# Gathering 64 more columns of v, splitting the weights of two blocks at once, and own homes for the first raw tile and the row of norms, in a streaming-encoder trunk

## The chip, the cores and the metric

The kernel runs as one program on one core of a Trainium2 chip. The metric is device microseconds of one execution. TensorE (PE) does the matmuls and transposes, VectorE (DVE), ScalarE (ACT) and GpSimd (POOL) the rest; SyncE (SP) issues most of the DMAs, POOL issues the gathers that take their row numbers from memory.

## The reference

256 tokens of width 2048 pass one layer: a convolution and an S5 state space side by side, a cross attention to 256 memory tokens, then a PEER layer and a last RMSNorm. The change lies in PEER and what follows it:

```python
def peer(h, w_q, sub_keys, u_tab, v_tab):
    q = (h @ w_q)...                               # 8 heads, two halves each
    ...                                            # two top-16 per head, top-16 of their 256 sums
    idx = ...                                      # 8 heads x 16 experts of 16384 per token
    g = jax.nn.softmax(top_s, axis=-1)
    u = jnp.take(u_tab, it, axis=0)
    act = jax.nn.gelu(jnp.einsum("td,tkd->tk", xt, u))
    v = jnp.take(v_tab, it, axis=0)
    return jnp.einsum("tk,tkd->td", gt * act, v)

out = rms_norm(h + peer(...), final_norm_g)
```

Each token picks 128 of 16384 experts, and an expert is a row of `peer_u` and a row of `peer_v`, both 2048 wide.

## The kernel before

The program is built with a Tile framework whose scheduler sets the order of instructions on each engine by a timeline of its own; pools with a fixed number of buffers and semaphores do the rest. The 256 tokens are two halves of 128 (`tt` = 0, 1). By the trace, mixing and attention run from 0 to about 777 us, the query projection `peer_w_q` to 842, the dot products with u and the routing to about 1533, the stage on v to 2047, and the last norm from there to the end at 2063.

**Dot products with u.** The first 768 columns of all 16384 rows of `peer_u` are read as 128 blocks of 128 rows (`dense()`): SP loads `raw`, PE transposes it (L969), ACT copies it to `ut` (L971), PE multiplies it with `hnT`, the transposed tokens (L975). The other 1280 columns are gathered for the picked rows only (`dot()`): POOL issues 256 gathers (L928), DVE multiplies and sums each (L930). `hnT` is made on POOL by an addition (L798) and a multiplication with `rbf`, the row of norms (L799).

**The stage on v.** The first DC = 1472 columns go through PE: the sparse gate-times-activation weights stand as a dense matrix `W`, two tiles WA and WB (one for each token half) of 128 blocks of 128 x 128. For each block SP loads 128 rows of `peer_v` (`vr`); ACT casts it to fp32r (`vh`, L103) and DVE takes the remainder (`vl`, L104); the block's weights are split in the same way (`wh` on ACT, L1205, `wl` on DVE, L1206, once for WA and once for WB); and PE sums three products (wh·vh L1215, wl·vh L1216, wh·vl L1217) for two halves and three column chunks (512, 512, 448) in PSUM: 18 matmuls a block. The other GC = 576 columns are gathered for the picked rows: 256 gathers on POOL (L1180) into 6 buffers `v`, and for each an accumulation on DVE, `accg = v * coef + accg` (L1182), 128 for the first token half and then 128 for the second. In the text of the program about two gathers stand behind each block:

```python
        while done * NB < (b + 1) * (NTT * NSLOT + 8) and done < NTT * NSLOT:
            next(gathering)
            done += 1
```

**The end.** For each half the matmul sums are added to the residual (L1225, DVE), squared and summed on ACT (L1226, and L1227 for `accg`), reduced (L1228), turned into a reciprocal root (L110, L111), and the four column pieces are scaled (L1234 to L1237) and stored. `accg` of the second half is complete only when its last gathered row is in.

The tile WB is not filled until `dense()`; until then the top of it serves as space for routing tiles, cut off by `host(n)`.

Of the kernel before, what the change touches and what calls it, by code (L numbers as in the profile page):

```python
# [9 lines left out]
F32 = mybir.dt.float32  # L10
F32R = mybir.dt.float32r
# [3 lines left out]
AF = mybir.ActivationFunctionType  # L15
# [5 lines left out]
P = 128  # L21
T = 256
NTT = T // P
# [15 lines left out]
NSLOT = PH * TOPK  # L39
NB = 128  # L40
# [7 lines left out]
DU = KD * P  # L48
DG = D - DU
GROUPS = ((1, 1, 2, 2, 2), (2, 2, 2, 2))  # L50
GC = 576
GU = 64
DC = D - GC
COLS = [slice(c, min(c + 512, DC)) for c in range(0, DC, 512)]
NCH = len(COLS)
VG_BUFS = 6
VR_BUFS = 4
WL_POOL = 0
PQ_COLS = (128, 384, 512)
NWHOLE = 1  # L60
W_IN, W_K, W_V = True, True, True
# [17 lines left out]
def trunk(ctx, tc, a, out, dbg=None):  # L79
    nc = tc.nc  # L80
    V, S, G, PE, SY = nc.vector, nc.scalar, nc.gpsimd, nc.tensor, nc.sync
# [4 lines left out]
    consts = ctx.enter_context(tc.tile_pool(name="consts", bufs=1))  # L86
# [7 lines left out]
    eps_t = consts.tile([P, 1], F32, name="eps_t")  # L94
# [10 lines left out]

    def row_bcast(vec):
        return bass.AP(tensor=vec.tensor, offset=vec.offset, ap=[[0, P], [1, D]])

    def rstd_of(dst, ssq, n):
        S.activation(dst, ssq, AF.Sqrt, bias=eps_t[: dst.shape[0]], scale=1.0 / n)  # L110
# [38 lines left out]
    with ExitStack() as wctx:  # L149
# [71 lines left out]
        def run(g):  # L221
            for _ in g:
                pass
# [5 lines left out]
        with ExitStack() as mctx:  # L229
# [382 lines left out]
            for k in range(CW):  # L612
                for q in range(CQ):
                    src, o = cpad[:, q, k:k + T], accs[q // 4][:, q % 4, :]
# [131 lines left out]
        ffn = wctx.enter_context(tc.tile_pool(name="ffn", bufs=1, side="right"))  # L746
        wb_p = wbx.enter_context(tc.tile_pool(name="wb_p", bufs=1))
        WB = wb_p.tile([P, NB, P], F32, name="WB")
        spare = [NB * P]

        def host(n):
            spare[0] -= n
            return WB.rearrange("p b t -> p (b t)")[:, spare[0]:spare[0] + n]
# [7 lines left out]
        cands = host(2 * TOPK * TOPK)  # L761
        top_r = [host(n * PH * TOPK) for n in (2, 2, 2, 1, 2, 2)]
        sco = [host(PH * 2 * P).rearrange("p (h s n) -> p h s n", h=PH, s=2) for _ in range(NTT)][::-1]
        free_blocks = spare[0] // P

        pq_cols = [(sum(PQ_COLS[:i]), w) for i, w in enumerate(PQ_COLS)]

        def ev_pq(n, half, ps):
# [5 lines left out]
            for sd in range(2):  # L774
# [6 lines left out]
                for tt in range(NTT):  # L781
                    S.activation(sco[tt][:, hh:hh + nh, sd, :], ss[:, tt, :nh], AF.Copy, scale=rstd_f[:, tt:tt + 1])

        run(linear(fT, a["peer_w_q"], 0, PH * P, ev_pq, False, cols=pq_cols))
        r8 = small.tile([P, NTT], F32, name="r8")
        V.tensor_scalar(r8, rstd_f, float(CH), None, op0=ALU.mult)
# [2 lines left out]
        for tt in range(NTT):  # L789
            V.tensor_scalar(dg[:, tt, :], ident, r8[:, tt:tt + 1], None, op0=ALU.mult)  # L790
            PE.matmul(pr[:, tt * P:(tt + 1) * P], ones, dg[:, tt, :], start=tt == 0, stop=tt == 1,
                      skip_group_check=True)
        rbf = ffn.tile([P, T], F32, name="rbf", tag="qp", bufs=2)
        S.copy(rbf, pr)
        for n in range((KD + 3) // 4):
            w = min(KD - 4 * n, 4)
            o = hnT[:, 4 * n:4 * n + w, :]
# [162 lines left out]
    def dense():  # L960
        for b in range(NB):
            if b == NB // 2:
                while (1, len(GROUPS[1]) - 1) not in ready:
                    yield
            raw = lr_d.tile([P, DU], F32, name="raw", bufs=4)
            SY.dma_start(raw, a["peer_u"][b * P:(b + 1) * P, :DU])
            pt = psd.tile([P, KD, P], F32, name="ut")
            for k in range(KD):
                PE.transpose(pt[:, k, :], raw[:, k * P:(k + 1) * P], ident)  # L969
            ut = lr_d.tile([P, KD, P], F32, name="ut", bufs=2)  # L970
            S.copy(ut, pt)  # L971
            if b % 2 == 0:
                ps = psd.tile([P, 2, T], F32, name="sy")
            for k in range(KD):
                PE.matmul(ps[:, b % 2, :], ut[:, k, :], hnT[:, k, :], start=k == 0 and b % 2 == 0,  # L975
                          stop=k == KD - 1 and b % 2 == 1, skip_group_check=True)
            if b % 2:
                S.copy(W[0][:, :, b - 1:b + 1], ps[:, :, :P].rearrange("p b t -> p t b"))
                S.copy(by_token[:, b // (NB // 2), :, (b - 1) % (NB // 2):(b - 1) % (NB // 2) + 2],
                       ps[:, :, P:].rearrange("p b t -> p t b"))  # L980
            yield
# [214 lines left out]

    gathering = gathered()
    done = 0
    for b in range(NB):
        if b == TAIL_AT:  # L1200
            load_tail()
        wh = vs.tile([P, NTT, P], F32R, name="wh")
        wl = vs.tile([P, NTT, P], F32R, name="wl")
        for tt in range(NTT):
            S.copy(wh[:, tt, :], W[tt][:, b, :])  # L1205
            (G if tt < WL_POOL else V).tensor_sub(wl[:, tt, :], W[tt][:, b, :], wh[:, tt, :].bitcast(F32))  # L1206
        vr = vraw_p.tile([P, DC], F32, name="vr")
        SY.dma_start(vr, a["peer_v"][b * P:(b + 1) * P, :DC])
        vh = vs.tile([P, DC], F32R, name="vh")
        vl = vs.tile([P, DC], F32R, name="vl")  # L1210
        split(vh, vl, vr)
        for tt in range(NTT):
            for c, cs_ in enumerate(COLS):
                o = acc[tt][:, c, :cs_.stop - cs_.start]
                PE.matmul(o, wh[:, tt, :], vh[:, cs_], start=b == 0, stop=False)  # L1215
                PE.matmul(o, wl[:, tt, :], vh[:, cs_], start=False, stop=False)  # L1216
                PE.matmul(o, wh[:, tt, :], vl[:, cs_], start=False, stop=b == NB - 1)  # L1217
        while done * NB < (b + 1) * (NTT * NSLOT + 8) and done < NTT * NSLOT:
            next(gathering)
            done += 1  # L1220

    sts = [small.tile([P, NCH + 3], F32, name="rms_st") for _ in range(NTT)]
    for tt, st in enumerate(sts):
# [45 lines left out]
```

## Time and profile before

| | |
|---|---|
| time, three runs | 2063.14, 2064.15, 2064.17 us (median 2064.15) |
| the profiled execution | 2064.74 us, of which the span from first to last instruction is 2063.0 us |
| busy share of the span | PE 95%, PE's weight loads 82%, DVE 82%, ACT 48%, POOL 38% |
| DMA | 571.78 MB, mean 277 GB/s; about 338 GB/s in the v stage |
| last matmul ends, end of span | 2046.95 us, 2063.0 us |

All other times below are in us from the start of the span of that profiled execution. Busy shares are means over very different stages: the v stage alone (1533 to 2047 us) is a quarter of the span, and in its last 16 us PE is idle.

### The profile page before, as it was taken

The page shows a single profiled execution, that of the slowest core. Times are in us where ns is not written, and L with a number is a line of the kernel's source. Part 1 is how long each engine was busy: PE and PEld are TensorE (multiplying, and loading weights), DVE is VectorE, ACT ScalarE, POOL GpSimd, SP SyncE. Part 2 cuts the span into 40 slices and gives each one's busy share as a digit, 9 for nine tenths or more (in the row PEclk, how much of TensorE's full clock was granted, in tenths as well). Part 3 has the DMA queues.
Part 4 walks back from the last instruction along what each step waited for, and adds up shares of the span by engine and source line. Part 5 has one row for each costly group of instructions (what it writes and reads, how often), then busy time and mean ns, then how long its engine had stood idle before and what let it go on. Part 6 is the DMA issues. An engine that isn't in the chain of part 4 may idle for free.

```text
span 2063.0 us, 33320 instructions
## 1 busy us (share of the span) xinstructions
PE 1961.4 (95%) x12361; PEld 1684.1 (82%) x12379; DVE 1683.5 (82%) x2757; ACT 998.2 (48%) x1586; POOL 777.7 (38%) x589
## 2 busy tenths in 40 slices
PE   8899999999999998899999989989999999999996
PEld 7888886786899888788888878867678888888885
DVE  6699999895655557999976666889869899899998
ACT  5775665455544445333333323556564444444444
POOL 1011111000000003444445656453128677677775
PEclk9999999999999999999999999999999999999998
DMA  7888788757855568899999999888539999999996
GB/s 238 204 227 221 202 224 223 226 183 230 276 180 173 168 196 280 273 310 327 318 354 398 406 384 407 282 294 280 172 128 338 364 336 340 343 341 338 337 339 228
DMA packets 203108, 571.78 MB, mean 277 GB/s; under 512 B 31410, under 2 KB 39459, under 8 KB 202818
## 3 DMA queue, kind: packets, MB, share of 16 engines
q1 hardware_dynamic: 135810, 307.48, 44.1%
q0 software_dynamic: 67136, 262.18, 37.8%
q8 instruction: 97, 1.59, 0.3%
q14 instruction: 65, 0.53, 0.1%
HBM read 556.74 MB, written 12.85 MB: 276 GB/s over the span
## 4 chain that ended last, share of the span: by engine, by line
PE 55%; DVE 15%; issue 11%; DMA 9%; POOL 7%; ACT 2%; SPq 0%; POOLq 0%; DVEq 0%; ACTq 0%
PE acc L1216 8%; PE acc L1217 8%; PE acc L1215 8%; POOL u L928 6%; DVE u L930 5%; PE mm L206 4%; PE mm L205 4%; PE mm L207 3%; PE mm L216 3%; PE mm L214 3%; PE mm L215 3%; PE pw L1051 3%; DMA w_lo<-in_w_kv_mem 2%; PE y L1016 1%; DMA xc<-in_mem 1%
## 5 line engine op out<-in xcount | busy, mean ns | idle before, releaser
L1180 POOL DMA_INDIRECT v<-in_peer_v,vidx x256 | 391.2, 1528 | 182.8 <-DVE accg L1182 72.5
L930 DVE SCALAR_TENSOR_TENSOR u<-u,hnF 128x1280 f32<-128x1280 f32 x256 | 387.9, 1518 | 86.2 <-DMA u<-in_peer_u,uidx 85.5
L928 POOL DMA_INDIRECT u<-in_peer_u,uidx x256 | 295.8, 1156 | 330.2 <-DVE u L930 243.3
L975 PE MATMUL sy<-hnT,ut 128*128 128x256 f32 x1536 | 357.6, 385 | 15.4 <-ACT ut L971 15.4
L191 ACT CAST w_hi<-w_raw 128x1024 fp32r<-128x1024 f32 (+2 forms) x228 | 231.3, 1017 | 242.8 <-PE mm L207 118.2
L975 PEld LDWEIGHTS sy<-hnT,ut 128*128 128x128 f32 x1536 | 287.6, 193 | 56.5 <-ACT ut L971 20.7
L196 DVE TENSOR_TENSOR w_lo<-w_raw,w_hi 128x1024 fp32r<-128x1024 f32 (+2 forms) x192 | 226.7, 1183 | 111.4 <-ACT w_hi L191 111.2
L103 ACT CAST vh<-vr 128x1472 fp32r<-128x1472 f32 x128 | 183.3, 1432 | 251.7 <-PE acc L1216 250.2
L1216 PE MATMUL acc<-vh,wl 128*128 128x512 f32 (+1 forms) x768 | 295.4, 385 | 0.3 <-DVE wl L1206 0.3
L1217 PE MATMUL acc<-vl,wh 128*128 128x512 f32 (+1 forms) x768 | 293.7, 385 | 0.1
L216 PE MATMUL mm<-aT_hi,w_lo 128*128 128x256 f32 x960 | 271.9, 290 | 18.8 <-DVE w_lo L196 7.5
L1215 PE MATMUL acc<-vh,wh 128*128 128x512 f32 (+1 forms) x768 | 276.0, 384 | 2.4 <-ACT vh L103 2.4
L214 PE MATMUL mm<-aT_hi,w_hi 128*128 128x256 f32 x960 | 277.1, 291 | 0.8 <-ACT w_hi L191 0.8
L215 PE MATMUL mm<-aT_lo,w_hi 128*128 128x256 f32 x960 | 274.4, 288 | 0.0
L104 DVE TENSOR_TENSOR vl<-vr,vh 128x1472 fp32r<-128x1472 f32 x128 | 216.8, 1694 | 41.9 <-ACT vh L103 41.4
L1182 DVE SCALAR_TENSOR_TENSOR accg<-v,coef,accg 128x576 f32<-128x576 f32 x256 | 208.7, 815 | 6.5 <-DMA v<-in_peer_v,vidx 2.5
L216 PEld LDWEIGHTS mm<-aT_hi,w_lo 128*128 128x128 f32 x960 | 182.8, 193 | 25.2 <-DVE w_lo L196 9.0
L214 PEld LDWEIGHTS mm<-aT_hi,w_hi 128*128 128x128 f32 x960 | 185.7, 194 | 6.6 <-issue 3.7
L215 PEld LDWEIGHTS mm<-aT_lo,w_hi 128*128 128x128 f32 x960 | 186.1, 194 | 3.4 <-issue 2.0
L1216 PEld LDWEIGHTS acc<-vh,wl 128*128 128x128 f32 x768 | 144.6, 188 | 30.9 <-DVE wl L1206 0.7
L1215 PEld LDWEIGHTS acc<-vh,wh 128*128 128x128 f32 x768 | 144.8, 188 | 28.3 <-ACT vh L103 2.6
L1217 PEld LDWEIGHTS acc<-vl,wh 128*128 128x128 f32 x768 | 144.5, 188 | 22.5 <-DVE vl L104 0.9
(383 smaller groups left out, 3187.8 us busy)
## 6 DMA issues: line engine op xcount, KB each, us to landing
vr<-in_peer_v SPq DMA_DIRECT2D x128, 736.0 KB
raw<-in_peer_u SPq DMA_DIRECT2D x128, 384.0 KB
w_raw<-in_w_kv_mem SPq DMA_DIRECT2D x64, 512.0 KB
w_raw<-in_w_in SPq DMA_DIRECT2D x48, 512.0 KB
w_raw<-in_w_out SPq DMA_DIRECT2D x32, 512.0 KB
w_raw<-in_w_q_mem SPq DMA_DIRECT2D x32, 512.0 KB
w_raw<-in_w_o_mem SPq DMA_DIRECT2D x32, 512.0 KB
w_lo<-in_w_kv_mem POOLq DMA_DIRECT2D x24, 512.0 KB, 7.9
```

The source lines that it names most:

```text
L191: S.copy(hi, raw)
L196: V.tensor_sub(lo, raw, hi.bitcast(F32))
L214: PE.matmul(o, wh, ah, start=first and cb % 2 == 0, stop=False, skip_group_check=True)
L215: PE.matmul(o, wh, al, start=False, stop=False, skip_group_check=True)
L216: PE.matmul(o, wl, ah, start=False, stop=last and end, skip_group_check=True)
L928: G.indirect_dma_start(out=u, out_offset=None, in_=a["peer_u"].rearrange("e (q c) -> (e q) c", c=GU), in_offset=bass.IndirectOffsetOnAxis( ...
L930: V.scalar_tensor_tensor(u, u, 1.0, hnF[:, self.tt, :], op0=ALU.mult, op1=ALU.mult, accum_out=self.act[:, j:j + 1])
L975: PE.matmul(ps[:, b % 2, :], ut[:, k, :], hnT[:, k, :], start=k == 0 and b % 2 == 0, stop=k == KD - 1 and b % 2 == 1, skip_group_check=True)
L1180: G.indirect_dma_start(out=v, out_offset=None, in_=table, in_offset=bass.IndirectOffsetOnAxis(ap=vidx[tt][:, j:j + 1], axis=0))
L1215: PE.matmul(o, wh[:, tt, :], vh[:, cs_], start=b == 0, stop=False)
L1216: PE.matmul(o, wl[:, tt, :], vh[:, cs_], start=False, stop=False)
L1217: PE.matmul(o, wh[:, tt, :], vl[:, cs_], start=False, stop=b == NB - 1)
```

## The change

- **64 columns move.** GC 576 becomes 640, so DC 1472 becomes 1408: each block of `vr`, `vh`, `vl` is 64 columns narrower, the last chunk of the matmuls has 384 columns in place of 448, and each gather and each `accg` is 64 columns wider. The numbers of all these instructions stay.
- **Weights two blocks at once (WGROUP = 2).** `wh` and `wl` become one tile for each half and two blocks, three buffers each: two casts and two subtractions of 256 columns for two blocks, in place of four of 128.
- **The order of the last blocks' products.** Those of the second half for the last two blocks stand behind everything else (`late`).
- **Quota of gathers.** `+ 8` becomes `+ 16` in the loop that emits gathers.
- **Homes.** `raw0`, the first `raw` block, and `rbf` get space in WB; `raw0` is loaded ahead of the `peer_w_q` projection. Before, `rbf` took a buffer of the tag "qp" of the projection.
- **`eps_j`.** One small square-root activation on ACT is written at TAIL_AT, where the loads for the last norm are issued.

```diff
-GC = 576
+GC = 640
...
-WL_POOL = 0
+WGROUP = 2
...
+    eps_j = consts.tile([P, 1], F32, name="eps_j")
...
-        free_blocks = spare[0] // P
+        raw0, rbf = host(DU), host(T)
...
+        SY.dma_start(raw0, a["peer_u"][:P, :DU])
         run(linear(fT, a["peer_w_q"], 0, PH * P, ev_pq, False, cols=pq_cols))
...
-        rbf = ffn.tile([P, T], F32, name="rbf", tag="qp", bufs=2)
...
-            raw = lr_d.tile([P, DU], F32, name="raw", bufs=4)
-            SY.dma_start(raw, a["peer_u"][b * P:(b + 1) * P, :DU])
+            if b:
+                raw = lr_d.tile([P, DU], F32, name="raw", bufs=4)
+                SY.dma_start(raw, a["peer_u"][b * P:(b + 1) * P, :DU])
+            else:
+                raw = raw0
...
+    def products(b, tt, wh, wl, vh, vl):
+        for c, cs_ in enumerate(COLS):
+            o = acc[tt][:, c, :cs_.stop - cs_.start]
+            PE.matmul(o, wh, vh[:, cs_], start=b == 0, stop=False)
+            PE.matmul(o, wl, vh[:, cs_], start=False, stop=False)
+            PE.matmul(o, wh, vl[:, cs_], start=False, stop=b == NB - 1)
+
+    late = []
     for b in range(NB):
         if b == TAIL_AT:
             load_tail()
-        wh = vs.tile([P, NTT, P], F32R, name="wh")
-        wl = vs.tile([P, NTT, P], F32R, name="wl")
-        for tt in range(NTT):
-            S.copy(wh[:, tt, :], W[tt][:, b, :])
-            (G if tt < WL_POOL else V).tensor_sub(wl[:, tt, :], W[tt][:, b, :], wh[:, tt, :].bitcast(F32))
+            S.activation(eps_j, eps_t, AF.Sqrt)
+        i = b % WGROUP
+        if i == 0:
+            wh, wl = ([vs.tile([P, WGROUP, P], F32R, name=nm, bufs=3) for _ in range(NTT)] for nm in ("wh", "wl"))
+            for tt in range(NTT):
+                w = W[tt][:, b:b + WGROUP, :]
+                S.copy(wh[tt], w)
+                V.tensor_sub(wl[tt], w, wh[tt].bitcast(F32))
...
-        for tt in range(NTT):
-            for c, cs_ in enumerate(COLS):
-                o = acc[tt][:, c, :cs_.stop - cs_.start]
-                PE.matmul(o, wh[:, tt, :], vh[:, cs_], start=b == 0, stop=False)
-                PE.matmul(o, wl[:, tt, :], vh[:, cs_], start=False, stop=False)
-                PE.matmul(o, wh[:, tt, :], vl[:, cs_], start=False, stop=b == NB - 1)
-        while done * NB < (b + 1) * (NTT * NSLOT + 8) and done < NTT * NSLOT:
+        products(b, 0, wh[0][:, i, :], wl[0][:, i, :], vh, vl)
+        if b < NB - 2:
+            products(b, 1, wh[1][:, i, :], wl[1][:, i, :], vh, vl)
+        else:
+            late.append((b, 1, wh[1][:, i, :], wl[1][:, i, :], vh, vl))
+        while done * NB < (b + 1) * (NTT * NSLOT + 16) and done < NTT * NSLOT:
             next(gathering)
             done += 1
+    for x in late:
+        products(*x)
```

The scheduler orders the built programs anew, and the text of the program does not tell how. Three places follow; a row that ends in "x2" stands for two equal instructions.

DVE, some blocks near the end of the v stage, before (two blocks; `accg_14570` is the second half's):

```order
L104 TENSOR_TENSOR vl<-vr,vh 128x1472
L1206 TENSOR_TENSOR wl<-WA,wh 128x128
L1206 TENSOR_TENSOR wl<-WB,wh 128x128
L1182 SCALAR_TENSOR_TENSOR accg_14570<-v,coef_8417,accg_14570 128x576 x2
L104 TENSOR_TENSOR vl<-vr,vh 128x1472
```

and after, from one block with two accumulations to the next one (L1223 is the new `wl`, L1187 the accumulation):

```order
L1187 SCALAR_TENSOR_TENSOR accg_14569<-v,coef_8418,accg_14569 128x640
L104 TENSOR_TENSOR vl<-vr,vh 128x1408
L1187 SCALAR_TENSOR_TENSOR accg_14569<-v,coef_8418,accg_14569 128x640 x2
L104 TENSOR_TENSOR vl<-vr,vh 128x1408
L1187 SCALAR_TENSOR_TENSOR accg_14569<-v,coef_8418,accg_14569 128x640
L1223 TENSOR_TENSOR wl<-WB,wh 128x256
L1223 TENSOR_TENSOR wl<-WA,wh 128x256
```

Before, two accumulations stand between any two `vl`, 16 in 8 blocks; now there are 14 in 8. So 248 of the 256 accumulations stood ahead of the last `vl` on DVE, and now 220 do.

DVE, the very end, before (L1237 scales and gives the output, L1228 reduces the second half's sums of squares, which need the last `accg`):

```order
L1237 SCALAR_TENSOR_TENSOR WA<-accg_14569,rms_st,WA 128x576
L1237 SCALAR_TENSOR_TENSOR WA<-WA,rms_st 128x512 x2
L1182 SCALAR_TENSOR_TENSOR accg_14570<-v,coef_8417,accg_14570 128x576
L1228 TENSOR_REDUCE rms_st<-rms_st 128x1
L111 RECIPROCAL rms_st<-rms_st 128x1
L1237 SCALAR_TENSOR_TENSOR WB<-accg_14570,rms_st,WA 128x576
L1237 SCALAR_TENSOR_TENSOR WB<-WB,rms_st,WA 128x512 x2
```

and after (L1255 is the former L1237, L1246 the former L1228):

```order
L1255 SCALAR_TENSOR_TENSOR WA<-accg_14568,rms_st,WA 128x640
L1255 SCALAR_TENSOR_TENSOR WA<-WA,rms_st 128x512 x2
L1187 SCALAR_TENSOR_TENSOR accg_14569<-v,coef_8418,accg_14569 128x640 x30
L1246 TENSOR_REDUCE rms_st<-rms_st 128x1
L113 RECIPROCAL rms_st<-rms_st 128x1
L1255 SCALAR_TENSOR_TENSOR WB<-accg_14569,rms_st,WA 128x640
L1255 SCALAR_TENSOR_TENSOR WB<-WB,rms_st,WA 128x512 x2
```

Where one accumulation stood between the first half's output and the second half's reduction, 30 stand now. Six more stand among the additions of the end, as seven did before.

POOL, at the query projection, before (L860 belongs to the routing, L928 are the gathers of u):

```order
L798 TENSOR_TENSOR hnT<-aT_hi_7052,aT_lo_7056 128x512
L860 TENSOR_TENSOR WB<-WB 128x256 x2
L928 DMA u<-in_peer_u,uidx 128x1280 x9
L860 TENSOR_TENSOR WB<-WB 128x256
L928 DMA u<-in_peer_u,uidx 128x1280
L860 TENSOR_TENSOR WB<-WB 128x256
L928 DMA u<-in_peer_u,uidx 128x1280 x2
L799 TENSOR_TENSOR hnT<-hnT,rbf 128x1024
L799 TENSOR_TENSOR hnT<-hnT,rbf 128x512
```

and after (L801 is the former L799, and `rbf` is now a part of WB):

```order
L800 TENSOR_TENSOR hnT<-aT_hi_7053,aT_lo_7057 128x512
L801 TENSOR_TENSOR hnT<-hnT,WB 128x1024
L801 TENSOR_TENSOR hnT<-hnT,WB 128x512
L862 TENSOR_TENSOR WB<-WB 128x256 x2
L930 DMA u<-in_peer_u,uidx 128x1280 x9
```

The multiplication with the norms moves from behind the first 12 gathers to the place right behind the addition. On SP the load of `raw0` stands ahead of both loads of `hnF`, among the last loads of `peer_w_q`. On ACT the activation of `eps_j` stands not at TAIL_AT but among the first instructions of the program.

## Rows read from the trace of the kernel before

**Rows 1.** Windows (start:end, length, busy us of PE PEld DVE ACT POOL, clock, DMA, GB/s)

```profile
1550.00:2040.00 490.00, 490.00 (x2215) 415.55 (x2214) 445.49 (x612) 225.02 (x371) 372.51 (x244) 1.00 0.94 338
```

**Rows 2.** Timeline of PE, one block period of the v stage, and the last matmul

```profile
2010.91 0.63 PE L1215 MATMUL acc<-vh,wh 128*128 128x512 f32 x2
...
2012.52 0.36 PE L1215 MATMUL acc<-vh,wh 128*128 128x448 f32 x1
...
2013.13 0.39 PE L1216 MATMUL acc<-vh,wl 128*128 128x512 f32 x1
...
2014.90 0.63 PE L1215 MATMUL acc<-vh,wh 128*128 128x512 f32 x2
...
2046.59 0.36 PE L1217 MATMUL acc<-vl,wh 128*128 128x448 f32 x1
```

**Rows 3.** Windows, a stretch of the attention's linear layer with 256-column matmuls

```profile
600.00:640.00 40.00, 40.00 (x337) 40.00 (x336) 23.70 (x35) 20.42 (x31) 0.00 (x0) 1.00 0.58 195
```

**Rows 4.** Groups by shape, DVE, 1550 to 2040 us (count | busy, mean ns | idle before)

```profile
L104 DVE TENSOR_TENSOR vl<-vr,vh 128x1472 fp32r<-128x1472 f32 x123 | 208.3, 1694 | 38.8 <-ACT vh L103 38.3
L1182 DVE SCALAR_TENSOR_TENSOR accg<-v,coef,accg 128x576 f32<-128x576 f32 x243 | 198.1, 815 | 4.4 <-DMA v<-in_peer_v,vidx 0.5
...
L1206 DVE TENSOR_TENSOR wl<-WA,wh 128x128 fp32r<-128x128 f32 x123 | 35.4, 288 | 1.3 <-ACT wh L1205 1.3
```

**Rows 5.** Timeline of DVE at the end of the v stage and behind it

```profile
2042.30 2.52 DVE L1182 SCALAR_TENSOR_TENSOR accg<-v,coef,accg 128x576 f32<-128x576 f32 x3
2045.22 1.82 DVE L1225 TENSOR_TENSOR WA<-WA,acc 128x512 f32<-128x512 f32 x3 [0.41 <-PE acc L1217]
...
2047.69 1.81 DVE L1225 TENSOR_TENSOR WB<-WB,acc 128x512 f32<-128x512 f32 x3
...
2054.91 0.81 DVE L1182 SCALAR_TENSOR_TENSOR accg<-v,coef,accg 128x576 f32<-128x576 f32 x1
```

**Rows 6.** The page's costliest groups: the 1280-column multiplication of u

```profile
L930 DVE SCALAR_TENSOR_TENSOR u<-u,hnF 128x1280 f32<-128x1280 f32 x256 | 387.9, 1518 | 86.2 <-DMA u<-in_peer_u,uidx 85.5
```

**Rows 7.** Timeline of POOL, gathers at the start of the v stage

```profile
1538.79 0.95 POOL L1180 DMA_INDIRECT v<-in_peer_v,vidx  x1 [0.31 <-issue]
...
1542.55 1.79 POOL L1180 DMA_INDIRECT v<-in_peer_v,vidx  x1 [0.30 <-issue]
```

**Rows 8.** Timeline of POOL, gathers of u at 1372 to 1384 us

```profile
1372.41 1.95 POOL L928 DMA_INDIRECT u<-in_peer_u,uidx  x1 [6.30 <-DVE u L930]
...
1383.52 1.50 POOL L928 DMA_INDIRECT u<-in_peer_u,uidx  x1 [0.30 <-issue]
```

**Rows 9.** Timeline of DVE over the same stretch

```profile
1373.47 1.49 DVE L930 SCALAR_TENSOR_TENSOR u<-u,hnF 128x1280 f32<-128x1280 f32 x1
...
1375.48 1.49 DVE L930 SCALAR_TENSOR_TENSOR u<-u,hnF 128x1280 f32<-128x1280 f32 x1
```

**Rows 10.** Timeline of POOL, gathers of v near the end of the stage

```profile
2037.11 1.70 POOL L1180 DMA_INDIRECT v<-in_peer_v,vidx  x1 [0.30 <-issue]
2039.39 1.40 POOL L1180 DMA_INDIRECT v<-in_peer_v,vidx  x1 [0.58 <-DVE accg L1182]
```

**Rows 11.** All gathers of line L1180, from issue to landing

```profile
DMA to landing us min/median/max: 3.9/6.7/9.9
```

**Rows 12.** Groups of PE, 842 to 1301 us (the dot products with u)

```profile
L975 PE MATMUL sy<-hnT,ut 128*128 128x256 f32 x1535 | 357.3, 385 | 15.4 <-ACT ut L971 15.4
L969 PE MATMUL ut<-ident,raw 128*128 128x128 f32 x768 | 104.1, 277 | 12.6 <-DMA raw<-in_peer_u 12.6
```

**Rows 13.** Timeline of PE, the longest waits for raw in that stage

```profile
847.24 2.79 PE L969 MATMUL ut<-ident,raw 128*128 128x128 f32 x12 [5.29 <-DMA raw<-in_peer_u]
...
1219.97 1.51 PE L969 MATMUL ut<-ident,raw 128*128 128x128 f32 x6 [6.32 <-DMA raw<-in_peer_u]
```

**Rows 14.** Timeline of POOL: the multiplication with the norms

```profile
841.59 3.57 POOL L799 TENSOR_TENSOR hnT<-hnT,rbf 128x1024 f32<-128x1024 f32 x2
```

**Rows 15.** Timeline of ACT: a wait near the program's start

```profile
19.46 0.64 ACT L253 ACTIVATE sqj<-xc 128x512 f32<-128x512 f32 x1 [4.33 <-DMA xc<-in_x]
```

## The prediction

> **What bounds the kernel now.** I read the windows by stage first. In the v stage PE is busy for all 490 us of a 490 us window, at the full clock (2.4 GHz of its two levels); DVE has 445, ACT 225 and POOL 373 us of work in the same time [rows 1]. So PE alone sets that stage. DVE is the runner-up, at 445.49 / 122.8 blocks = 3.63 us of a block of 3.99 us.
>
> The timeline of PE then gives the price of a matmul. A block's 18 matmuls repeat every 14.90 - 10.91 = 3.99 us; three of 448 columns take 13.13 - 12.52 = 0.61 us, so 0.2033 each; the twelve of 512 columns take (3.99 - 6 x 0.2033) / 12 = 0.2308 each [rows 2]. (The durations printed are longer, since neighbours overlap; starts count.) The slope is 0.0275 us for 64 columns. It doesn't end at 448: in an earlier linear layer 256-column matmuls go by at 40.00 / 337 = 0.1187 us each, weight loads included [rows 3], which gives (0.2308 - 0.1187) / 4 = 0.0280 for 64 columns. So 384 columns are on the same line.
>
> Behind the stage PE has nothing to do. Its last matmul ends at 2046.59 + 0.36 = 2046.95 us, which I call T [rows 2]; the span ends 16.05 us later. In the tail the DVE rows show what stands there: the additions of the second half at 2047.69, and the last accumulation at 2054.91 to 2055.72, then 7.3 us for reduction, root, scaling and store [rows 5]. Last comes the stage of the dot products with u, where PE is idle for 15.4 + 12.6 = 28.0 us, waiting for `ut` and `raw` [rows 12].
>
> **The change part by part.**
>
> *Narrower matmuls.* 128 blocks x 6 = 768 matmuls lose 64 columns: 768 x 0.0275 = 21.1 us (21.5 by the other slope) [rows 2, 3]. The block comes to 3.99 - 0.165 = 3.825 us. Can the others keep up? DVE has a `vl` of 1.694 x 1408 / 1472 = 1.62, at most 0.58 for the weights (one subtraction of 256 columns for two blocks and each half costs at most two of 128, at 0.288) and 14 / 8 accumulations a block [rows 4]. One of 640 columns takes 0.815 + 64 x (1518 - 815) / (1280 - 576) ns = 0.88 us [rows 4, 6]. Sum: 1.62 + 0.58 + 1.75 x 0.88 = 3.74 us, below 3.825 even without the overlap at the edges. DMA traffic falls from 736 + 2 x 288 = 1312 KB to 704 + 1.75 x 320 = 1264 KB a block, so the rate stays at about the 338 GB/s of [rows 1]. PE keeps the stage, and T comes 21.1 us earlier.
>
> *The order on DVE.* This term decides. 220 accumulations stand ahead of the last `vl`, where 248 stood, and 30 stand in one piece between the first half's output and the second half's reduction, where one stood. That DVE has 1.75 in place of 2 accumulations a block is what let the sum above close; the rest of the work is not gone, it stands behind T, where no matmul hides it. DVE executes its list in order, and the reduction needs the last accumulation.
>
> When does the run of 30 begin? The second half's additions could start 0.4 us after the last matmul, the wait that the first half's show; from the start of these additions to the accumulation that stands where the 30 now stand took 2054.91 - 2047.69 = 7.2 us [rows 5]. So it begins at T + 7.6. Each accumulation follows the one before it at (2.52 - 0.815) / 2 = 0.853 us [rows 4, 5], plus 64 columns' 0.064: 0.92 us. On DVE alone the run takes 30 x 0.92 = 27.6 us and ends at T + 35.2.
>
> But their rows must be gathered too. There are six buffers, so six gathers have landed when the run begins and 24 can be issued only as buffers come free, the first at T + 8.8 (behind the first accumulation and the 0.3 us that POOL's rows show ahead of a gather). With a spacing s the last is issued at T + 8.8 + 23 s, lands 3.9 us later (the shortest of all gathers; the DMA rings have nothing else left) [rows 11], and its accumulation ends 0.92 us behind that: T + 13.6 + 23 s.
>
> What is s? No row shows gathers of v in a row beside nothing but accumulations. The lower end: at the start of the v stage, with DVE mostly waiting, three follow each other in 1542.55 - 1538.79, 1.25 us each [rows 7]. The upper end: gathers of u beside a DVE that is hardly ever free come at (1383.52 - 1372.41) / 6 = 1.85 us [rows 8], with DVE operations of 1.49 us behind each other there [rows 9]. In the tail DVE would be busy 0.92 of each s, between the two. Near the end of the v stage a gather holds POOL for 1.70 or 1.40 us (the latter next to accumulations) [rows 10]. I take s = 1.5: last accumulation at T + 48.1, end at T + 48.1 + 7.3 = T + 55.4. Before, the end was at T + 16.05, so the tail costs 39.4 us more. With s = 1.25 it is 33.6, with s = 1.85 it is 47.4, with DVE alone as the pace (T + 35.2 + 7.3) 26.4.
>
> The rows of gathers beside a busy DVE are longer (1.85 against 1.25), though the operations there read two SBUF tiles each [rows 7, 8, 9]. The Trainium skill (SBUF — State Buffer, Who interferes with whom) says that an operation with two SBUF inputs takes only the read side of the port pair that DVE shares with GpSimd, and infers that generating descriptors needs the write side, so that tensor_tensor wasn't seen to stall DMAs. By that rule the spacing would be the undisturbed 1.25 us and the time 2074.2; by the rows it may be up to 1.85 and 2088.0.
>
> *First raw tile, `rbf`, order on POOL.* PE begins the dot products with u 5.29 us late, waiting for the first `raw` [rows 13]. With `raw0` there early that wait goes, but the next block's `raw` waits for the same pool as before, so what is left is about one block: 459 us / 128 = 3.6, less a little for what the earlier start meets. The multiplication with the norms sat at 841.59 to 845.16 on POOL [rows 14], which would now be the next to be late (the product needs it); it is moved ahead of the gathers, so it isn't. There it occupies POOL for 3.6 us, ahead of the first gathers of u, and it can hold up DVE's routing work beside it. I take -3; bounds: +1 (the routing is delayed, the wait only moves), and -8.6 (first wait, and half of the 6.32 us one at 1219.97 [rows 13], gone too).
>
> *`eps_j`.* It stands at the start of ACT, not at the end where it could have moved anything; its table load is hidden in waits like ACT's 4.33 us for input at 19.46 [rows 15]. Nothing; at most 1.3 us if that cover is gone.
>
> *`late`, the split by twos on ACT.* Nothing: PE does the same matmuls, and the first half's additions come earlier, but the 30 accumulations set the end.
>
> *Sum*, against the profiled execution's own 2064.74 us (0.6 above the median of 2064.15): 2064.74 - 21.1 - 3 + 39.4 = **2080.0 us**.
>
> **The rivals.** About 0.2% (4.1 us) is what a measurement of this kernel can tell from no change.
>
> *A, the forecast*: the run of 30 is paced by its gathers, s between 1.25 and 1.85: 2064.74 - 24.1 + 33.6 = 2074.2 to 2064.74 - 24.1 + 47.4 = 2088.0. For it: 24 of the 30 can't be issued before buffers come free, and no row shows gathers closer than 1.25. Chance 0.70, and 0.06 more for the case that the middle gives nothing (the change's homes don't do what they are for): 2083.0, inside the same range.
>
> *B, DVE alone paces the run*: gathers are issued as fast as accumulations free buffers. 2064.74 - 24.1 + 26.4 = 2067.0, no measurable change. Against it: it takes a spacing of 0.92, under every row. It could come nearer if more of the 36 accumulations slip in while DVE waits for PE's last products, but the order is fixed. Chance 0.12.
>
> *C, faster*: the stage of the dot products with u, where PE is idle for 28.0 us [rows 12], runs without a break because the first tile and the multiplication no longer come late and the whole chain of `raw`, `ut` and gate shifts. 2064.74 - 21.1 - 28.0 + 39.4 = 2055.0. It decides from 39.4 - 21.1 = 18.3 us saved there, 22.4 for a measurable gain. Against it: only one 5.29 us wait of these is the first tile's; 15.4 us of them are waits for `ut`, which the change doesn't touch. Chance 0.04 (with the lowest tail, 26.4, it would need 5.3, or 9.4 us for a measurable gain, just beyond my bound for the middle; another 0.01).
>
> *D, slower still*: DVE, at 3.74 of 3.825 us, becomes the bound in blocks with two accumulations (1.62 + 0.58 + 1.76 = 3.96), and 0.1 us a block adds to the tail: 128 x 0.1 = 13 us, 2093. Against it: six buffers and two blocks' lead even out over 8 blocks. Chance 0.07.
>
> **How the numbers follow.** Likeliest is A with s = 1.5: 2080.0. From 2066.5 to 2090 the range takes in A, B and the case without a middle gain; C and D, 0.12, lie outside. Faster by over 0.2%: C, 0.05. Within 0.2% (2060.0 to 2068.3): B, 0.12. Slower: A, its poorer case and D, 0.83.
>
> **What would show it.** In the profile after: matmul starts of a block 3.82 to 3.83 us apart, with the last chunk at 0.176 each; PE's last matmul near 2046.95 - 24.1 = 2022.8; then on DVE one row of 30 accumulations (or rows broken by waits on the gathers' DMA), beginning 7 to 8 us after the last matmul and lasting 35 to 47 us, where PE's slices are empty; POOL with 24 gathers 1.25 to 1.85 us apart in the same stretch; the end 7.3 us behind the last accumulation. In the middle: no 5.29 us wait of the first transposes, and a wait for the second `raw` in its place. I am wrong if the gathers of the tail come at 1 us, if the accumulations turn out to be done before the last matmul, or if PE's blocks are longer than 3.85 us.

## The result, and the profile after

The changed kernel takes 2083.66 us (median of 7 runs, 2073.85 to 2091.02); the kernel before takes 2064.15 beside it. The ratio is 1.0098, 95% interval [1.0079, 1.0117]: slower by one per cent. The profiled execution was the slowest of the seven, 2091.02 us with a span of 2089.2.

In this profile the timeline of PE has the narrow matmuls and the last one (start, duration, instruction):

```profile
2019.65 0.34 PE L1208 MATMUL acc<-vh,wh 128*128 128x384 f32 x1
2019.83 0.34 PE L1209 MATMUL acc<-vh,wl 128*128 128x384 f32 x1
2020.00 0.58 PE L1210 MATMUL acc<-vl,wh 128*128 128x384 f32 x2
...
2029.14 0.34 PE L1210 MATMUL acc<-vl,wh 128*128 128x384 f32 x1
```

Matmuls of 384 columns come 0.175 us apart. The first matmul of the stage starts at 1536.45 (row further down), so the stage took 2029.48 - 1536.45 = 493.03 us. Before, the first one and the reduction of the second half's sums (on DVE) stood here:

```profile
1533.99 0.74 PE L1215 MATMUL acc<-vh,wh 128*128 128x512 f32 x1 [2.39 <-ACT vh L103]
2056.57 0.16 DVE L1228 TENSOR_REDUCE rms_st<-rms_st 128x1 f32<-128x4 f32 x1 [0.84 <-ACT WB L1227]
```

The stage took 2046.95 - 1533.99 = 512.96 us then, so PE saved 19.9 us. The timeline of DVE shows where they went, and 24 more:

```profile
2030.52 1.74 DVE L1243 TENSOR_TENSOR WB<-WB,acc 128x512 f32<-128x512 f32 x3
...
2036.39 1.41 DVE L1255 SCALAR_TENSOR_TENSOR WA<-WA,rms_st 128x512 f32<-128x512 f32 x2
2037.71 5.48 DVE L1187 SCALAR_TENSOR_TENSOR accg<-v,coef,accg 128x640 f32<-128x640 f32 x6
2043.61 0.89 DVE L1187 SCALAR_TENSOR_TENSOR accg<-v,coef,accg 128x640 f32<-128x640 f32 x1 [0.41 <-DMA v<-in_peer_v,vidx]
2045.33 0.89 DVE L1187 SCALAR_TENSOR_TENSOR accg<-v,coef,accg 128x640 f32<-128x640 f32 x1 [0.83 <-DMA v<-in_peer_v,vidx]
...
2081.11 0.89 DVE L1187 SCALAR_TENSOR_TENSOR accg<-v,coef,accg 128x640 f32<-128x640 f32 x1 [0.86 <-DMA v<-in_peer_v,vidx]
2082.89 0.16 DVE L1246 TENSOR_REDUCE rms_st<-rms_st 128x1 f32<-128x4 f32 x1 [0.90 <-ACT WB L1245]
```

Six accumulations run back to back, since their rows lay in the six buffers; each of the other 24 waits for its gather. The reduction, 9.6 us behind the last matmul before, now stands 53.4 us behind it. POOL in the same stretch (first, second and last of the 24 gathers):

```profile
2038.86 1.47 POOL L1185 DMA_INDIRECT v<-in_peer_v,vidx  x1 [1.57 <-DVE accg L1187]
2040.63 1.54 POOL L1185 DMA_INDIRECT v<-in_peer_v,vidx  x1 [0.30 <-DVE accg L1187]
...
2076.66 1.25 POOL L1185 DMA_INDIRECT v<-in_peer_v,vidx  x1 [0.30 <-issue]
```

They are (2076.66 - 2038.86) / 23 = 1.64 us apart. Two more places, on PE: the start of the dot products with u, where [rows 13] showed a wait of 5.29 us, and the start of the v stage:

```profile
847.12 1.51 PE L974 MATMUL ut<-ident,WB 128*128 128x128 f32 x6 [0.98 <-ACT WB L784]
849.67 4.79 PE L980 MATMUL sy<-hnT,ut 128*128 128x256 f32 x12 [1.03 <-ACT ut L976]
854.29 1.47 PE L974 MATMUL ut<-ident,raw 128*128 128x128 f32 x12
856.00 2.86 PE L980 MATMUL sy<-hnT,ut 128*128 128x256 f32 x12 [0.23 <-ACT ut L976]
...
1215.95 1.51 PE L974 MATMUL ut<-ident,raw 128*128 128x128 f32 x6 [7.15 <-DMA raw<-in_peer_u]
...
1536.45 0.79 PE L1208 MATMUL acc<-vh,wh 128*128 128x512 f32 x1 [2.24 <-ACT vh L103]
```

### The profile page after: what moved, and what is told of

The parts are those of the page before. It is cut to its first block, busy times and chain, and to the rows that moved or that the text cites. A ratio compares the mean times of both kernels' runs of the same rounds, so it can differ in the third digit from the quotient of the medians.

```text
span 2089.2 us, 33010 instructions
## 1 busy us (share of the span) xinstructions
PE 1944.8 (93%) x12361; PEld 1676.4 (80%) x12379; DVE 1682.0 (81%) x2629; ACT 988.5 (47%) x1460; POOL 746.9 (36%) x589
## 4 chain that ended last, share of the span: by engine, by line
PE 53%; DVE 16%; issue 13%; POOL 8%; DMA 8%; ACT 2%; POOLq 0%; SPq 0%; DVEq 0%; ACTq 0%
PE acc L1208 8%; PE acc L1210 8%; PE acc L1209 8%; POOL u L930 6%; DVE u L932 5%; PE mm L208 3%; PE mm L209 3%; PE mm L207 3%; PE mm L218 3%; PE mm L216 3%; PE mm L217 3%; PE pw L1056 3%; DMA w_lo<-in_w_kv_mem 3%; POOL v L1185 1%; DVE w_lo L198 1%
## 5 line engine op out<-in xcount | busy, mean ns | idle before, releaser
L1185 POOL DMA_INDIRECT v<-in_peer_v,vidx x256 | 362.9, 1418 | 240.3 <-DVE accg L1187 145.1
L1208 PE MATMUL acc<-vh,wh 128*128 128x512 f32 (+1 forms) x768 | 289.0, 376 | 2.2 <-ACT vh L103 2.2
L1209 PE MATMUL acc<-vh,wl 128*128 128x512 f32 (+1 forms) x768 | 288.1, 375 | 0.0
L1210 PE MATMUL acc<-vl,wh 128*128 128x512 f32 (+1 forms) x768 | 278.0, 375 | 0.0
L1187 DVE SCALAR_TENSOR_TENSOR accg<-v,coef,accg 128x640 f32<-128x640 f32 x256 | 225.4, 881 | 19.1 <-DMA v<-in_peer_v,vidx 17.6
L103 ACT CAST vh<-vr 128x1408 fp32r<-128x1408 f32 x128 | 175.9, 1374 | 134.1 <-PE acc L1209 126.7
L104 DVE TENSOR_TENSOR vl<-vr,vh 128x1408 fp32r<-128x1408 f32 x128 | 208.1, 1625 | 36.8 <-ACT vh L103 33.2
L976 ACT COPY ut<-ut 128x768 f32<-128x768 f32 x128 | 100.3, 800 | 172.9 <-PE ut L974 154.4
```

Source lines behind the costliest of these rows:

```text
L1185: G.indirect_dma_start(out=v, out_offset=None, in_=table, in_offset=bass.IndirectOffsetOnAxis(ap=vidx[tt][:, j:j + 1], axis=0))
L1208: PE.matmul(o, wh, vh[:, cs_], start=b == 0, stop=False)
L1209: PE.matmul(o, wl, vh[:, cs_], start=False, stop=False)
L1210: PE.matmul(o, wh, vl[:, cs_], start=False, stop=b == NB - 1)
```

## The experiments

All figures of a stage come from the PE timeline of each profile: the first matmul of the v stage, the end of its last, and the end of the span (the tail is what lies between the last two). Each ratio is to the kernel before, timed beside that run (2064.09 to 2065.84 us).

| kernel | v stage starts | its length | tail | time, ratio to before [95%] |
|---|---|---|---|---|
| before | 1534.0 | 513.0 | 16.1 | 2064.15 |
| changed | 1536.5 | 493.0 | 59.7 | 2083.66, 1.0098 [1.0079, 1.0117] |
| e1_hand | 1528.0 | 530.4 | 13.8 | 2079.11, 1.0073 [1.0047, 1.0098] |
| e2_gc640_alone | 1531.7 | 496.7 | 55.1 | 2087.92, 1.0114 [1.0089, 1.0139] |
| e3_all_but_gc | 1536.7 | 512.5 | 18.0 | 2064.08, 0.9997 [0.9982, 1.0012] |
| e4_homes | 1532.7 | 512.7 | 16.9 | 2062.39, 0.9982 [0.9966, 0.9999] |
| e5_two_by_hand | 1525.8 | 653.6 | 13.8 | 2202.55, 1.0661 [1.0638, 1.0684] |
| e6_hold | 1528.0 | 654.8 | 63.2 | 2247.66, 1.0880 [1.0846, 1.0914] |
| e7_hold_no_gather | 1530.2 | 651.9 | 45.0 | 2229.98, 1.0800 [1.0772, 1.0829] |
| e8_hold_no_accumulate | 1529.4 | 652.0 | 45.5 | 2228.67, a single run |
| e9_one_by_hand | 1524.4 | 506.9 | 13.8 | 2049.32, 0.9928 [0.9907, 0.9949] |
| e10_two_four_buffers | 1529.9 | 516.0 | 13.8 | 2060.99, 0.9976 [0.9962, 0.9989] |
| e11_changed_again | 1525.3 | 493.1 | 59.5 | 2082.61, 1.0084 [1.0067, 1.0102] |
| e12_one_exact_quota | 1526.4 | 500.1 | 13.8 | 2047.77, 0.9928 [0.9910, 0.9947] |

**Which part of the change does it.** e2 is the kernel before with only the width; e3 the changed kernel without it; e4 the kernel before with only the homes.

```diff
 e2                        e3                        e4
-GC = 576                 -GC = 640                 +        raw0, rbf = host(DU), host(T)
+GC = 640                 +GC = 576                 +        SY.dma_start(raw0, a["peer_u"][:P, :DU])
```

> The kernel before with GC = 640 and nothing else of the change. On DVE the scheduler puts 223 accumulations ahead of the last vl, and 27 in one run ahead of the second half's reduction. Theory 1 (the width alone does it): 20 us less on PE, 23 gathers fewer than a full hiding, tail of 16 + 27 x 1.5 = about 55 us, time 2078 to 2086 us, as the whole change. Theory 2 (the split by twos, the late products or eps_j matter): time below 2070 us.

> The changed kernel with GC back at 576; all its other parts stay. The scheduler puts 245 accumulations ahead of the last vl and none in a long run behind it (before: 248). Theory 1: no tail, time 2060 to 2066 us, within 0.2% of before; the homes may give up to 4 us. Theory 2 (another part than the width makes the loss): above 2075 us.

> The kernel before with only the homes for the first raw tile and the row of norms. My prediction took 3 us of gain in the middle of the kernel, the trace of the change shows PE's way from the last query product to the end of the dot products with u 4.3 us shorter, but the v stage began 2.5 us later than before. If the 4.3 us hold and the lateness is something else: 2060 us, and the v stage begins near 1530. If the homes themselves cost what they give: 2064, beginning near 1534. If they make routing late: 2066 to 2067, beginning near 1536.5.

Timeline of DVE in e2, the run and what follows it (its last matmul ended at 2028.36):

```profile
2036.59 5.48 DVE L1182 SCALAR_TENSOR_TENSOR accg<-v,coef,accg 128x640 f32<-128x640 f32 x6
2042.50 0.88 DVE L1182 SCALAR_TENSOR_TENSOR accg<-v,coef,accg 128x640 f32<-128x640 f32 x1 [0.42 <-DMA v<-in_peer_v,vidx]
...
2075.39 0.88 DVE L1182 SCALAR_TENSOR_TENSOR accg<-v,coef,accg 128x640 f32<-128x640 f32 x1 [0.69 <-DMA v<-in_peer_v,vidx]
```

The width alone makes the whole loss: its tail is 55.1 us, with the same picture of six and then one by one, and its time lies a little beyond my 2086. Without it the time is that of before. The homes by themselves (e4) give 2062.39 against 2064.94, an interval from 0.01 to 0.34% of gain.

**Is it the order?** e1 keeps everything and takes DVE's v stage in the text's order.

```diff
     late = []
+    by_hand = ctx.enter_context(ExitStack())
+    by_hand.enter_context(tc.manual_schedule(engines={mybir.EngineType.DVE}))
     for b in range(NB):
...
         products(*x)
+    by_hand.close()
```

> The changed kernel with one difference: in the v stage DVE takes its instructions in the order of the program's text (two accumulations behind each vl), so that all 256 accumulations stand ahead of the last matmuls; nothing is left out. Theory 1 (the scheduler's order on DVE, which leaves 36 accumulations behind the last vl, makes the loss): the last matmul stays near 2029.5 us, the end comes about 16 us behind it as before, span about 2046 and time about 2047 us, 36 us faster than the changed kernel and 17 faster than before. Theory 2 (DVE has no room for two accumulations of 640 columns a block): the blocks grow to 3.9 to 4.0 us, the last matmul ends near 2040 to 2047 us, time 2057 to 2065 us. Theory 3 (the loss lies in the middle or in the split by twos): time stays near 2080 us.

The tail went from 59.7 to 13.8 us, as theory 1 had it, but the v stage grew from 493.0 to 530.4 us, and the time fell by less than 5 us. Timelines of DVE, then of ACT, in e1:

```profile
1811.94 0.42 DVE L1225 TENSOR_TENSOR wl<-WA,wh 128x256 fp32r<-128x256 f32 x1
1813.13 0.47 DVE L1225 TENSOR_TENSOR wl<-WB,wh 128x256 fp32r<-128x256 f32 x1 [0.77 <-ACT wh L1224]
```

```profile
1812.69 0.41 ACT L1224 CAST wh<-WB 128x256 fp32r<-128x256 f32 x1 [1.13 <-PE acc L1210]
```

DVE waits for `wh`, and `wh` waits for PE to release a buffer. I then took ACT by hand too (e5), the weights of the next pair behind `vl` of the odd block and `eps_j` ahead of the loop; and in the same round, with that order as base, three kernels: 32 accumulations held back behind the first half's scaling (e6), the same with the last 26 gathers left out (e7), and with the accumulations of gathers 225 to 250 left out (e8).

```diff
 e5
-    by_hand.enter_context(tc.manual_schedule(engines={mybir.EngineType.DVE}))
+    by_hand.enter_context(tc.manual_schedule(engines={mybir.EngineType.DVE, mybir.EngineType.Activation}))
...
         split(vh, vl, vr)
+        if i == WGROUP - 1 and b < NB - 1:
+            nxt = weights(b + 1)
 e6, over e5
-        while done * NB < (b + 1) * (NTT * NSLOT + 16) and done < NTT * NSLOT:
+        while done < (b + 1) * 7 // 4:
...
+        if tt:
+            run(gathering)
         S.activation(sq[tt][:, DC:], accg[tt], AF.Square, accum_out=st[:, NCH:NCH + 1])
 e7, over e6
+                if tt * NSLOT + j < 230:
                     v = vg.tile([P, GC], F32, name="v")
 e8, over e6
+                if not 224 <= tt * NSLOT + j < 250:
                     V.scalar_tensor_tensor(accg[tt], v, coef[tt][:, j:j + 1], accg[tt], op0=ALU.mult, op1=ALU.add)
```

> The changed kernel with the order of both DVE and ACT in the v stage as in the program's text, and the text put in the order that the kernel before has: vl, then on every second block the weights of the next two, then two accumulations (with the DVE order alone, e1_hand, the accumulations were hidden but each pair of blocks lost time where wl on DVE waited for wh, which ACT had in the opposite order, and the v stage grew to 530 us). Nothing is left out. Theory 1 (order is all; DVE has room for two accumulations a block): a v stage of 492 to 496 us as in the changed kernel, tail of 14 to 16 us, time 2040 to 2046 us, a ratio of 0.989 to 0.992 to before. Theory 2 (DVE has no room): v stage of 505 us or more, time above 2053.

> As e5_two_by_hand, but with 7 gathers and accumulations for 4 blocks: 224 accumulations ahead of the last additions, and 32 in one run behind the first half's scaling; the order of the changed kernel made by hand. The small product of the last norm is one operation on DVE. Nothing is left out. If the run behind T is the loss: v stage of 493 us and a tail near 60 to 64 us, 2085 to 2092 us, within 8 us of the changed kernel. If something else in the scheduler's order is: well below 2075.

> As e6_hold, but the last 26 gathers are left out: their accumulations read the six buffers gathered last (so the second half's last 26 gathered terms are wrong). The run of 32 is then paced by DVE alone. Forecast A (gathers pace the run): 32 x 0.92 = 29.4 us for the run, tail of about 7.6 + 29.4 + 7.3 = 44 us, 17 us or so less than e6_hold. Rival B (DVE paces it): the same time as e6_hold within 3 us.

> As e6_hold, but the accumulations of gathers 225 to 250 are left out (26 gathered terms are missing); their gathers stay and are free to run ahead. It shows how far apart gathers come when DVE does no accumulations between them. If the accumulations set the 1.6 us spacing of the changed kernel's tail: 1.25 us apart where DVE is idle, as at the start of the v stage. If 1.6 us is the gather's own pace at 640 columns: 1.5 to 1.7 us here too.

e5 was wrong in a way that neither theory had: 653.6 us for the v stage. Its DVE, then its ACT:

```profile
1804.31 0.43 DVE L1217 TENSOR_TENSOR wl<-WB,wh 128x256 fp32r<-128x256 f32 x1 [4.06 <-ACT wh L1216]
1804.65 1.80 DVE L1187 SCALAR_TENSOR_TENSOR accg<-v,coef,accg 128x640 f32<-128x640 f32 x2
```

```profile
1803.87 0.41 ACT L1216 CAST wh<-WB 128x256 fp32r<-128x256 f32 x1 [8.07 <-PE acc L1210]
1804.18 2.64 ACT L103 CAST vh<-vr 128x1408 fp32r<-128x1408 f32 x2
```

ACT stands 8.07 us at `wh` with both `vh` queued behind it. The cause is in the change: the tiles of WA and WB carry the same name, so three buffers serve both, one and a half pairs of blocks; the second `wh` of a pair must wait until PE is through with the first of the pair before. In the changed kernel ACT waits for these buffers too, 131.2 us in all over the v stage, but PE is busy for 493.01 of its 493.05 us: the scheduler's order had placed each cast so that the wait cost nothing. Mine didn't.

e6 to e8 have the same long v stage, so their times miss what was expected of them; their tails are still good for the question that they were made for, since they lie behind that stage. DVE in e6 (the run begins and ends), DVE in e7, POOL in e8 (the first and the last of 17 gathers, DVE idle until 2212.29):

```profile
2190.95 6.41 DVE L1187 SCALAR_TENSOR_TENSOR accg<-v,coef,accg 128x640 f32<-128x640 f32 x7
...
2237.51 0.89 DVE L1187 SCALAR_TENSOR_TENSOR accg<-v,coef,accg 128x640 f32<-128x640 f32 x1 [0.76 <-DMA v<-in_peer_v,vidx]
```

```profile
2190.16 29.43 DVE L1192 SCALAR_TENSOR_TENSOR accg<-v,coef,accg 128x640 f32<-128x640 f32 x32
```

```profile
2193.21 0.95 POOL L1185 DMA_INDIRECT v<-in_peer_v,vidx  x1 [0.30 <-issue]
...
2213.22 0.94 POOL L1185 DMA_INDIRECT v<-in_peer_v,vidx  x1 [0.30 <-issue]
```

e6 reproduces the changed kernel's tail by hand: 63.2 us. Without the last gathers the same 32 accumulations take 29.43 us, 0.92 each, and the tail 45.0: gathers pace the run, and DVE alone would cost 18 us less. Without accumulations beside them the gathers come (2213.22 - 2193.21) / 16 = 1.25 us apart in place of 1.64.

**The shared buffers, and a better version.** e9 takes the order of e5 with the weights of one block at once and six buffers, e10 that of e5 with four buffers (and five for gathered rows), e12 is e9 with an even quota.

```diff
 e9, over e5                              e10, over e5
-WGROUP = 2                              -VG_BUFS = 6
+WGROUP = 1                              +VG_BUFS = 5
...
-        ... name=nm, bufs=3)             -        ... name=nm, bufs=3)
+        ... name=nm, bufs=6)             +        ... name=nm, bufs=4)
 e12, over e9
-        while done * NB < (b + 1) * (NTT * NSLOT + 16) and done < NTT * NSLOT:
+        while done * NB < (b + 1) * (NTT * NSLOT + 4) and done < NTT * NSLOT:
```

> As e5_two_by_hand, with WGROUP = 1 (the weights of one block at once) and six buffers each for wh and wl in place of three. In the changed kernel the tiles of both halves share one name and so three buffers, which is one and a half pairs of blocks; in e1_hand and e5_two_by_hand wh waited on ACT for PE to leave a buffer, with vh queued behind it. Nothing is left out. Theory 1 (that handshake made the 530 and 655 us; DVE has room for two accumulations of 640 columns a block, 1.54 + 0.42 + 1.72 = 3.68 of 3.83 us): v stage of 493 to 500 us, tail of 14 to 16, time 2040 to 2050 us. Theory 2 (DVE has no room): v stage above 505 us, time above 2055.

> As e5_two_by_hand, with four buffers in place of three for wh and wl, and five in place of six for the gathered rows, since the space ends there. Nothing is left out. Theory 1 (the shared buffers): the 655 us of the v stage fall to 495 to 510 us, time 2043 to 2058. Theory 2 (the order of ACT by hand is what costs): 650 us again.

> As e9_one_by_hand, with the quota of gathers at + 4 in place of + 16, which is 2.03 accumulations a block up to the last block but two in place of 2.125 up to the last block but seven. Nothing is left out. In e9 the v stage took 506.9 us with DVE busy for 95 to 97 of 100 us, and in its last blocks DVE waited 1.8 us a block. Theory 1 (DVE had become the bound there): the v stage falls by 0.094 x 0.86 = 0.08 us a block or some 9 us, to 496 to 500, and the time to 2038 to 2043 us, a ratio near 0.989. Theory 2 (the handshake of ACT, PE and DVE is what is left): v stage at 505 us or more, time 2047 or more.

Four buffers in place of three took the v stage from 653.6 to 516.0 us, with the order unchanged: the buffers were what the order met. My range for it (495 to 510) was too low; whether five buffers for gathered rows or 2.125 accumulations a block took the rest stays open, though from 1540 to 2000 us DVE waited 30.3 us for gathered rows there and 10.3 in e9, which has six. e9 has the stage at 506.9, over the 493 to 500 of theory 1 and over theory 2's 505 as well, but its time of 2049.32 us is the one that theory 1 gave, and it beats both kernels. One window of 100 us in e9, and the same in e12 (PE, PEld, DVE, ACT, POOL):

```profile
1800.00:1900.00 100.00, 99.16 (x465) 84.75 (x464) 95.67 (x131) 45.17 (x78) 78.26 (x56) 1.00 0.98 365
```

```profile
1800.00:1900.00 100.00, 100.00 (x471) 86.21 (x470) 96.94 (x132) 46.23 (x79) 84.02 (x53) 1.00 0.98 362
```

With 2.03 accumulations a block PE is not idle in this window, nor anywhere from 1600 to 2000 us, and the stage took 500.1 us in the profile, at the edge of theory 1. Of the 7.1 us that it has over the changed kernel's 493.0, 5.1 are one wait near its start (timeline of PE in e12):

```profile
1537.97 0.79 PE L1210 MATMUL acc<-vl,wh 128*128 128x512 f32 x1 [5.13 <-DVE vl L104]
```

The times of e9 and e12 (0.9928 each) can't be told apart, though; the 2038 to 2043 expected of e12 is not what the median shows, only its profiled run (2042.08).

**The spread.** e11 is the changed kernel again.

> The changed kernel once more, unaltered, for its spread (2073.85 to 2091.02 us in seven runs; the profiled one was the slowest). If the tail's spacing of gathers varies from execution to execution: a profile with another time has another spacing, 0.1 us for every 2.3 us of time. If the earlier stages vary: the spacing stays near 1.63 us and the v stage begins earlier or later.

Its 24 gathers are 1.63 us apart, its v stage takes 493.1 us and its tail 59.5: nothing of the spread is there. The spans differ by 11.3 us, and 11.2 of that is the start of the v stage. 200 to 600 us, in the profile of the change, then in e11:

```profile
200.00:400.00 200.00, 190.71 (x1286) 155.82 (x1285) 177.92 (x281) 119.66 (x152) 24.16 (x20) 0.97 0.80 212
400.00:600.00 200.00, 193.08 (x1058) 164.29 (x1057) 148.42 (x228) 102.11 (x135) 3.62 (x3) 0.97 0.69 221
```

```profile
200.00:400.00 200.00, 193.70 (x1308) 157.35 (x1307) 184.18 (x292) 121.18 (x154) 24.15 (x20) 0.98 0.81 217
400.00:600.00 200.00, 193.16 (x1099) 165.90 (x1098) 146.27 (x228) 105.44 (x141) 3.62 (x3) 0.99 0.68 221
```

e11 has 22 and 41 matmuls more in these two stretches. The granted clock is 0.97 and 0.97 in the profile of the change against 0.98 and 0.99 there; as an estimate, if PE sets the pace in them (it is busy for 191 to 194 of 200 us), 0.01 and 0.02 of 200 us make about 6 of the 11 us. The rest isn't assigned.

## Why the prediction was right

**The decisive step**, that 30 accumulations in one piece behind the last matmul cost more than the matmuls save, held. The tail grew by 43.6 us; the run of 30 took 44.3 (2037.71 to 2082.00), where one accumulation of 0.8 had stood, and what lies before and behind it is as long as it was, within 0.3 us. That the order on DVE makes this tail is shown by e1 (that order changed and nothing else, tail 13.8) and e6 (such an order made by hand, tail 63.2).

**The sum** came nearer to the result than its terms did. Against the profiled execution, 2091.02, from which the terms are read, 2080.0 is 11.0 us short: 1.2 in the matmuls, 4.2 in the tail, 5.5 in the middle, all on one side. That the median of 2083.66 lies only 3.7 away is luck: in e11 (2079.69) the v stage and the tail are as long as in that profile, and the v stage began 11.2 us earlier, 8.1 of it already at the first query product, in stages that no term of the sum is about.

**The tail** was 39.4 in the sum and measured 59.7 - 16.05 = 43.6. Its terms: the run began 8.2 us behind T, not 7.6; the gathers' spacing was 1.64, not 1.5 (over 23 spacings 37.8 us and not 34.5, the largest part); the last gather's row was used 4.45 us after its issue, not 3.9. The value of 1.5 was a choice between two rows, and the prediction had no mechanism for it; the last section has one. Each accumulation took the 0.92 us worked out from the 576-column rows (e7: 29.43 / 32). Rival B is excluded by e7.

**Matmuls.** 21.1 forecast, 19.9 measured. The 384-column matmuls are on the line (0.175), but from 1600 to 2000 us `vl` starts on DVE every 3.987 us before and every 3.832 us after: a block got shorter by 0.155 us, not by 0.165, which over 128 blocks is the difference of about 1.2 us.

**DVE keeps up** held at 1.75 accumulations a block, so rival D is out. With 2.125 (e9) PE was idle for 4.1 of the 400 us from 1600 to 2000, with 2.03 (e12) for none of them.

**The middle** was mis-sized, and of the wrong sign in the profile: -3 forecast, the v stage began 2.5 us later. The first wait did go, from 5.29 us to 0.98. The wait for the second `raw`, forecast in its place, did not come: the next wait for a `raw` is at 1215.95. PE reached the second `raw` only at 854.29 because the 12 products ahead of it took 4.79 us, where the next 12 took 2.86. Windows of these two stretches (the clock is the third number from the end):

```profile
849.67:854.46 4.79, 4.79 (x14) 3.85 (x15) 4.62 (x18) 0.00 (x0) 1.88 (x2) 0.59 0.81 261
854.46:858.00 3.54, 3.31 (x21) 2.86 (x20) 3.44 (x9) 1.51 (x2) 0.94 (x1) 1.00 0.98 237
```

The granted clock was 0.59 in the first, behind PE's waits of 0.98 and 1.03 us, so mostly at the lower of its two levels (1.2 and 2.4 GHz), and 1.00 in the second. The lateness of the v stage is made up of three pieces. 4.2 us stood already at the first query product (794.5 against 790.3), ahead of everything that the homes touch, and such differences come and go between executions of one program (e11: 786.4). From the last query product to the last dot product with u it is 459.3 before and 455.0 after, yet 454.3 in e2, which has no homes. From there to the v stage it is 233.0 before and 235.6 after, yet 232.9 in e11. So the traces can't show this term; the timed runs of e4 put it between 0.2 and 7 us of gain.

**`eps_j` and `late`** at nothing: e3 has both, with the homes and the split by twos, and is at 0.9997. What each of them does by itself is not shown.

## What to carry to other kernels

In this kernel, moving columns from matmuls to gathers pays only if the gathers' consumers stay under the matmuls, and in a scheduled program that is decided by the order that the scheduler finds anew, not by the quota in the text: read the order near the end of the loop before believing a slope. A tile name that two halves share halves the buffers; that doesn't show while the order happens to fit, and cost some 140 us in e5 (v stage of 653.6 us with three buffers, 516.0 with four). Here the same width with the accumulations in step and buffers for every tile took 0.7% off the kernel before, where the change as it stood cost 1.0%.

## What the runs showed of the hardware

Issuing a gather of 128 rows held POOL for 0.95 us with 0.30 between two, at 640 columns (e8) as at 576 [rows 7], when no operation of DVE held it up. In the tail of the changed kernel, with one accumulation of 0.92 us for each, gathers came 1.64 us apart. Which operations hold a gather up, the timelines of POOL show, read beside those of DVE; here two gathers of the changed kernel, then one of e8 with the accumulation that began beside it:

```profile
2030.87 0.94 POOL L1185 DMA_INDIRECT v<-in_peer_v,vidx  x1 [1.13 <-DVE accg L1187]
2045.62 1.42 POOL L1185 DMA_INDIRECT v<-in_peer_v,vidx  x1 [0.30 <-issue]
```

```profile
2211.97 0.94 POOL L1185 DMA_INDIRECT v<-in_peer_v,vidx  x1 [0.30 <-issue]
2212.29 0.88 DVE L1188 SCALAR_TENSOR_TENSOR accg<-v,coef,accg 128x640 f32<-128x640 f32 x1 [22.76 <-DMA v<-in_peer_v,vidx]
```

- The gather at 2045.62 was issued while the accumulation of 2045.33 ran, which ended at 2046.22, 0.60 us later. It took 1.42 us, 0.47 more than 0.95.
- The one at 2030.87 was issued while the additions of 2030.52 ran. One of their inputs, `acc`, lies in PSUM. It took 0.94.
- The one of e8 was already under way when the accumulation began. It took 0.94.

All 256 gathers of v in the changed kernel follow this. 163 were issued while an operation with both inputs in SBUF was running, begun at least 0.06 us before and with over 0.13 us left: they took 0.95 us plus what was left beyond the 0.13, to within 0.03 us. The other 93, two of them beside additions from PSUM, took 0.94 to 0.95. So the spacing in the tail follows from where in an accumulation each gather is issued.

The Trainium skill (SBUF — State Buffer, Who interferes with whom) says that a DVE operation with two inputs in SBUF contends with a GpSimd instruction that reads SBUF and not with one that only writes it, and infers that making descriptors needs the write side. The prediction took from the inference that gathers would stay 1.25 us apart; these runs decide against that reading. They don't contradict the rule on reads, since a gather also reads its row numbers from `vidx` in SBUF. Which part of a gather waits is not shown.
